# Output projection and Fourier feature products in scaled 16-bit halves, with the next layer's first weights made beside the projection

## The chip, the cores and the metric

The program runs on one core of a Trainium2 chip. The metric is the time of one execution on the device in microseconds (us); for a kernel it is the median of several runs. A profile is taken of one execution, and its span is the time from that execution's first instruction to its last. The engines are PE (TensorE: matmuls, with weight loads as PEld), DVE (VectorE), ACT (ScalarE), POOL (GpSimd) and SP (SyncE, which here issues every DMA).

## The reference

Two layers of a diffusion backbone run over 2048 latent tokens `x` and 256 context tokens `y`, with 1024 features. Each layer:

```
shift, scale, gate = split(silu(c) @ w_mod[l] + b_mod[l], 3)        # and the same from c_ctx for the context
h = rmsnorm(x, norm_g[l]) * (1 + scale) + shift
f_in, f_gate, g_u, g_v, g_gate, c_q, c_kv, k_rope, a_gate = split(h @ w_in[l])
f = (real(fft2(f_in by 4 groups of 64 features)) @ w_fmix[l]) * silu(f_gate)
g = spatial_gate(g_u, g_v) * silu(g_gate)                            # chunks of 128 tokens
o = attention(q(c_q), k, v(c_kv, k_rope)) * silu(a_gate)             # 8 heads, keys: context + latent
x = x + gate * (concat(f, g, o) @ w_out[l])                          # 256 + 256 + 512 features
```

The context takes the same step in the first layer only, with attention among itself. The output is `x` of the second layer, in 32-bit floats. `w_out` is 1024 x 1024 per layer, `w_fmix` 256 x 256, `w_mod` 1024 x 3072.

## The kernel before

The 2304 tokens are 18 tiles of 128 tokens (2 of the context, then 16 latent ones). Each operand of a matmul that must be exact is kept as a high and a low part, and a product is three matmuls: high x high, high x low, low x high (`mm3`, before line 682). For most of the kernel the parts are 16-bit floats: a matrix is first multiplied by a power of two that brings its largest entry near a fixed exponent (`power`, line 664, which needs a transpose, some tiny VectorE steps and a small matmul), then `halve` (line 866) makes the high part with two ScalarE passes and the low part with one POOL subtraction. The output projection and one step of the Fourier transform instead use pairs of 32-bit "f32r" tiles made by `split` (line 689): a ScalarE copy, and a subtraction on VectorE or POOL.

A layer has three stages:

1. Input projections, over blocks of two to six tiles. The columns of `w_in` are made into five weight groups (`group`, `resident`); group 0 holds keys and 416 columns, group 2 the gMLP's part. Each tile is normalised (`norm`) and transposed into 16-bit halves; the modulation is already multiplied into the small vectors `gs` and `sh`, made by `modulate_turned`, 64 VectorE operations for two of the three parts of `w_mod` (two conditions). Each takes 512 columns of a weight row and adds to an accumulator; `bounded` then fixes a power of two for the layer.
2. Attention over 8 heads, in steps of four query tiles. For each pair of key tiles a score matmul goes into PSUM, its maxima are scanned by VectorE, ScalarE takes two exponentials, POOL (three pieces of four) or VectorE (one of four) makes the low part, and PE multiplies by the values. Beside it a generator `background()` (line 1706) is advanced by fixed counts: first `fourier` (products by 64-point and 2048-point transforms, then by `w_fmix`), then the gate part (part 2) of `modulate_turned`, then `gates`, then `prepare` for the next layer.
3. The output stage. `weights()` (line 1005) loads `w_out` in two column halves of eight 128 x 512 pieces each through three buffers `wf`, and splits each to `wh` and `wl`. For each token tile, `mixed` (line 965) loads the concatenated mix from DRAM in three pieces into a buffer `k5`, transposes it (8 transposes in 2 groups, tiles `cb` and `cx`) and splits it. `outward` (line 1664) loads 512 columns of x, calls `project` (line 1027: 8 x 3 matmuls of 128 x 512 into a PSUM tile `pj`), multiplies by the gate, adds x and stores. Six tiles are made ahead (`XB`); between halves, two steps of the next layer's `modulate_turned` (parts 0 and 1) run, with 8 buffers `mw`.

The order of the instructions is not the order of the code. Every call is recorded and then a planner gives each engine a list in order of program priority, by an estimate of costs and by the number of free buffers in its pools; an instruction may be taken ahead of its place if its inputs and buffers are there. Each engine then runs its list strictly in that order, and all DMAs go through SyncE in 8 lanes. Every instruction is emitted by one line (448 before, 450 after), so the profile's rows are told apart by the names of tiles: `sc` scores, `pp` and `pw` exponentials, `pj` projections, `mw` weight rows of the modulation, `wf` raw pieces of `w_out`, `k` a general 32-bit buffer, `h` stacked halves (in the order also `h9`, `hp`).

Attention runs from 640 to 1427 us in layer 0 and from about 2180 to 2929 in layer 1; the output stages follow it, to 1686 and to the end.

Of the kernel before, what the change touches and what calls it, by code (L numbers as in the profile page):

```python
# [21 lines left out]
P = 128  # L22
D = 1024
# [38 lines left out]
XB = 6  # L62
# [4 lines left out]
PTOP, CTOP = 29, 14  # L67
# [482 lines left out]
def hybrid_kernel(ctx: ExitStack, tc: tile.TileContext, a: dict, out: bass.AP):  # L550
# [33 lines left out]
    def large():  # L584
        return mk(main, [P, T], F32R, "h9", 6)

# [3 lines left out]
    def k5():  # L590
        return mk(main, [P, NT * 65], F32, "k5")
# [96 lines left out]

    def split(hi, lo, x, leng=None):
        act.activation(out=hi, in_=x, func=AF.Copy)  # L690
        (leng or dve).tensor_tensor(out=lo, in0=x, in1=f(hi), op=ALU.subtract)
# [225 lines left out]
    def operand():  # L917
        h = large()
        parts = h[:, :2 * D].rearrange("p (s k n) -> p s k n", s=2, k=KC)
        return parts[:, 0], parts[:, 1]  # L920

# [42 lines left out]

    def mixed(t):
        xt = k5()[:, :D]
# [11 lines left out]
        return hh, hl  # L978
# [26 lines left out]
    def weights(parts, wp, scale=None, extra=None):  # L1005
        n = sum(c for _, c in parts)
        wt = []
        for k in range(KC):
            wf = mk(wp, [P, NB], F32, "wf", WF)[:, :n]
            c0 = 0  # L1010
            for get, c in parts:
                get(k, wf[:, c0:c0 + c])
                c0 += c
            if extra and k >= WB - KC:
                wh, wl = (mk(extra, [P, NB], F32R, s, 2 * KC - WB) for s in ("wh", "wl"))
            else:
                wh, wl = (mk(wp, [P, NB], F32R, s, WB)[:, :n] for s in ("wh", "wl"))
            if scale is not None and k >= 4:
                v = scale[:, k - 4:k - 3]
                act.activation(out=wh, in_=wf, func=AF.Copy, scale=v)  # L1020
                dve.scalar_tensor_tensor(out=wl, in0=wf, scalar=v, in1=f(wh), op0=ALU.mult, op1=ALU.subtract)
            else:
                split(wh, wl, wf, pool if k % 2 else dve)
            wt.append((wh, wl))
        return wt

    def project(ht, wt, n):
        o = bank(tag="pj")
        hh, hl = ht
# [242 lines left out]
    def fourier(l, y, pf):  # L1272
        back = mk(pf, [P, 1], F32, "back", 1)
        dve.tensor_scalar(out=back, in0=y["ic"][1], scalar1=2.0 ** (PTOP - CTOP), scalar2=None, op0=ALU.mult)
        fm = mk(pf, [P, 6, 256], F32R, "fm", 1)
        wfm = mk(pf, [P, 4, 256], F32, "wfm", 1)
        sp.dma_start(out=wfm, in_=a["w_fmix"][l].rearrange("k p n -> p k n"))
        first = wfm[:, 0]
        flip = column(C_FLIP)
        for s in range(3):  # L1280
# [4 lines left out]
            split(fm[:, 2 * s], fm[:, 2 * s + 1], first, pool)  # L1285
            yield

        def finish(re, im, cs, views):
# [22 lines left out]
            sh_ = [mk(pf, [P, 2, P], F32R, f"st{q}") for q in range(2)]  # L1311
            split(sh_[0], sh_[1], o)
            for gate_rows, out_rows, w in views:
                if w == 4:
                    sr_ = [mk(pf, [P, 2, P], F32R, f"sr{q}", 1) for q in range(2)]
                    for s, r in zip(sh_, sr_):
                        dve.tensor_copy(out=r, in_=f(s)[:, :, ::-1])
# [345 lines left out]
    def outward(l, y, t, n, ht, wt):  # L1663
# [6 lines left out]
        dve.tensor_tensor(out=o, in0=o, in1=y["gr"][1 if t < CT else 0][:, ns], op=ALU.mult)  # L1670
# [29 lines left out]
    for l in range(DEPTH):  # L1700
# [4 lines left out]
        def background():  # L1705
# [6 lines left out]
            load = lambda: mk(pools["W"], [P, NB], F32, "wh", WB)  # L1712
            for _ in modulate_turned(l, y, (2,), load):
                for _ in range(PACE):
                    yield
            gates(l, y, pools["C"])
# [162 lines left out]
```

## Time and profile before

| what | value |
|---|---|
| median of 3 runs | 3146.82 us (3145.03 to 3150.45) |
| profiled execution | 3142.39 us, span 3140.6 us |
| mean granted TensorE clock | 0.973 |
| DMA | 289.08 MB in 487,865 packets, 92 GB/s on average |
| HBM | 193.18 MB read, 91.66 MB written |

A row of a group gives the line, the engine, the operation, the output and inputs by name and shape, the count, then busy time in us and the mean ns of one, then the idle time of the engine just before them and what ended most of it. A row of the timeline gives the start, the duration and in square brackets the idle time before. A row of windows gives the length of a stretch, the busy time of each engine with its instruction count, the granted clock, the share of time in which a DMA engine was busy, and GB/s. "PEclk" is the TensorE clock that was granted, as a share of full speed.

### The profile page before, as it was taken

The numbers are of one execution on the slowest core, as the hardware profiler recorded it, in microseconds if no ns is written. First come the engines' busy times: TensorE is split into PE (matmuls) and PEld (weight loads), VectorE is DVE, ScalarE is ACT, GpSimd is POOL, SyncE is SP. The second block draws the span as 40 slices with busy tenths as digits, with TensorE's granted clock in tenths as the row PEclk, the third lists the DMA queues.
The fourth block names the chain that finished last, engine by engine and source line by source line (L and its number), as shares of the span: only waits on it lengthen the run. The fifth ranks groups of instructions, "written<-read, shape, count | busy, mean of one in ns | idle before, by whom it ended". The sixth has DMA issues, their size and how long they took to land.

```text
span 3140.6 us, 64404 instructions
## 1 busy us (share of the span) xinstructions
PE 2953.2 (94%) x23194; PEld 1724.2 (55%) x23194; DVE 2458.5 (78%) x6740; ACT 1826.3 (58%) x3904; POOL 1693.5 (54%) x1836
## 2 busy tenths in 40 slices
PE   6789999899999999998999999998999999999899
PEld 3445555445554555556785454553555555555687
DVE  7878788789999978765638888887899989887332
ACT  4553444167777788883006644531887887888400
POOL 3564444357667777772004744542876777777300
PEclk8899999999999999999999999998999999999999
DMA  7333344422324322205535343345023241230342
GB/s 271 69 73 58 84 94 87 102 88 67 86 61 131 81 72 61 57 23 177 175 118 192 62 86 86 87 96 142 24 64 79 71 125 49 61 75 20 111 134 81
DMA packets 487865, 289.08 MB, mean 92 GB/s; under 512 B 372316, under 2 KB 424180, under 8 KB 487544
## 3 DMA queue, kind: packets, MB, share of 16 engines
q1 hardware_dynamic: 487544, 284.96, 35.1%
q8 instruction: 182, 2.98, 0.4%
q14 instruction: 139, 1.14, 0.1%
HBM read 193.18 MB, written 91.66 MB: 91 GB/s over the span
## 4 chain that ended last, share of the span: by engine, by line
PE 59%; DVE 20%; DMA 8%; ACT 6%; POOL 3%; issue 2%; SPq 2%; DVEq 0%; ACTq 0%; POOLq 0%
PE pj L448 20%; PE sc L448 16%; PE pv L448 10%; PE mx L448 9%; DVE k L448 6%; DVE mx L448 4%; PE cb L448 3%; DMA k<-d 2%; ACT k L448 2%; SPq L448 2%; POOL k L448 2%; ACT pp L448 1%; DVE ns_t L448 1%; DMA mw<-in_w_modT_dram 1%; ACT pw L448 1%
## 5 line engine op out<-in xcount | busy, mean ns | idle before, releaser
L448 POOL TENSOR_TENSOR pp<-pw,pp 128x512 f16<-128x512 f32 (+1 forms) x876 | 1021.0, 1183 | 395.9 <-ACT pw L448 317.6
L448 PEld LDWEIGHTS <-h 128*128 128x128 f16 (+2 forms) x7008 | 581.8, 98 | 772.2 <-issue 410.2
L448 DVE TENSOR_REDUCE mx<-mx 128x1 f32<-128x512 f32 (+1 forms) x1296 | 770.9, 626 | 142.9 <-PE mx L448 136.9
L448 ACT ACTIVATE pp<-sc 128x512 f16<-128x512 f32 (+1 forms) x1168 | 717.5, 615 | 228.8 <-PE sc L448 215.5
L448 PE MATMUL sc<-h,h 128*128 128x512 f16 (+1 forms) x2336 | 602.8, 380 | 4.1 <-ACT pw L448 1.7
L448 ACT ACTIVATE pw<-sc 128x512 f32<-128x512 f32 (+1 forms) x876 | 543.7, 621 | 0.6 <-POOL pp L448 0.6
L448 PEld LDWEIGHTS <-pp 128*128 128x128 f16 x10432 | 467.3, 98 | 115.1 <-issue 32.5
L448 PE MATMUL pv<-k,pp 128*128 128x65 f16 (+2 forms) x10432 | 507.6, 203 | 7.6 <-DVE sm L448 7.0
L448 PE MATMUL mx<-h,h 96*128 96x512 f16 (+1 forms) x1296 | 410.4, 366 | 34.9 <-DVE mx L448 25.5
L448 PE MATMUL pj<-wh,h 128*128 128x512 f32 x1088 | 361.9, 405 | 7.3 <-DVE k L448 7.1
L448 PEld LDWEIGHTS <-hp 128*128 128x128 f16 x1920 | 187.8, 99 | 176.0 <-issue 14.3
L448 PE MATMUL pj<-w,h 128*128 128x512 f16 (+1 forms) x1296 | 272.2, 349 | 4.8 <-DVE tm L448 3.6
L448 PE MATMUL pj<-w,hp 128*128 128x512 f16 (+1 forms) x1152 | 241.4, 347 | 8.5 <-DVE tm L448 4.5
L448 POOL TENSOR_TENSOR h<-k,h 128x512 f16<-128x512 f32 (+1 forms) x72 | 80.8, 1138 | 299.6 <-ACT h L448 298.4
L448 PEld LDWEIGHTS pj<-wh,h 128*128 128x128 f32 x1088 | 208.6, 192 | 56.7 <-DVE k L448 11.1
L448 DVE TENSOR_TENSOR pp<-sc,pp 128x512 f16<-128x512 f32 (+1 forms) x292 | 197.8, 677 | 42.6 <-ACT sc L448 39.7
L448 PE MATMUL sc<-h 40*128 40x512 f16 (+1 forms) x1168 | 228.2, 387 | 0.0
L448 PE MATMUL pj<-wl,h 128*128 128x512 f32 x544 | 216.8, 399 | 0.0
L448 PE MATMUL pj<-h,h 128*128 128x416 f16 (+2 forms) x912 | 201.7, 363 | 6.5 <-ACT h L448 5.0
L448 DVE TENSOR_TENSOR pj<-pj,gr 128x512 f32<-128x512 f32 x68 | 47.3, 698 | 187.3 <-PE pj L448 187.3
L448 PE MATMUL pj<-h,hp 128*128 128x512 f16 (+1 forms) x768 | 174.4, 365 | 6.4 <-ACT hp L448 3.3
L448 ACT ACTIVATE sc<-sc 128x512 f32<-128x512 f32 (+1 forms) x292 | 178.8, 612 | 0.0
(270 smaller groups left out, 3936.7 us busy)
## 6 DMA issues: line engine op xcount, KB each, us to landing
d<-k SPq DMA_DIRECT2D x560, 48.0 KB
d<-k SPq DMA_DIRECT2D x166, 128.0 KB
d<-k SPq DMA_DIRECT2D x70, 256.0 KB
k<-d SPq DMA_DIRECT2D x132, 128.0 KB
k<-d SPq DMA_DIRECT2D x66, 256.0 KB
h<-d SPq DMA_DIRECT2D x24, 432.0 KB
d<-vt SPq DMA_DIRECT2D x144, 65.0 KB
k<-d SPq DMA_DIRECT2D x16, 585.0 KB
```

The lines of the kernel that those rows point to most:

```text
L448: r = getattr(getattr(self.nc, eng), method)(*args, **kw)
```

## The change

`weights()`, `operand()` and `split()` go. In their place:

- Weights of the output projection. `output_weights` runs at the end of `background()`, in attention: 16 loads of `w_out` pieces into one resident tile `wo` of 16-bit halves (each piece first sits there in full 32 bits), 16 VectorE maxima, `power`, then 16 `halve` calls. It is advanced once in three steps (`OPACE`).
- Tiles of the mix. `mixed` now scales each token tile by a power of two from its sum of squares: a ScalarE square with accumulation over 1024 columns, six VectorE steps on one column, a ScalarE scaling in place, then transposes as before and 16-bit halves, of two tiles in one `stacked` buffer. The inverse scale is applied in `outward`, in the operation that multiplies by the gate. The tiles made ahead fall from 6 to 4, the buffers `k5` rise from 2 to 3.
- The next layer. `onward` makes modulation parts 0 and 1 with 6 buffers `mw` in the pool W, `bounded`, and then the weight groups 0 and 2 in a new pool G, beside the output projection, in steps of 2 and 1 (`TICKS`) behind the two halves of a tile. All tiles do both halves in turn.
- Fourier. `w_fmix` is scaled and kept in 16-bit halves `fm`; the other operand `st` is 16-bit halves too, scaled by 2^-16. Its inverse scale is folded into `back`.

The core of the diff:

```diff
-TICKS = 2
+TICKS = 2, 1
+AHEAD_G = 2,
+OPACE = 3
-WB, WF = 11, 3
+WF = 3
-MW = 8
+MW = 6
-XB = 6
+XB = 4
...
     def k5():
-        return mk(main, [P, NT * 65], F32, "k5")
+        return mk(main, [P, NT * 65], F32, "k5", 3)
...
     def mixed(t):
         xt = k5()[:, :D]
...
-        hh, hl = operand()
+        ss = mk(small, [P, 1], F32, "ss")
+        act.activation(out=k2([P, D], BF16), in_=xt, func=AF.Square, accum_out=ss)
+        dve.tensor_scalar(out=ss, in0=ss, scalar1=2.0 ** -100, scalar2=2.0 ** 100, op0=ALU.max, op1=ALU.min)
+        pq = mk(small, [P, 2], F32, "mq", XB + 2)
...
+        dve.tensor_scalar(out=pq[:, 1:], in0=pq[:, 1:], scalar1=ow["pw"][:, 1:], scalar2=None, op0=ALU.mult)
+        act.activation(out=xt, in_=xt, func=AF.Copy, scale=pq[:, 0:1])
...
-            split(hh[:, 4 * half:4 * half + 4], hl[:, 4 * half:4 * half + 4], tp)
+            act.activation(out=hh[:, s], in_=tp, func=AF.Copy)
+            dve.tensor_tensor(out=hl[:, s], in0=tp, in1=hh[:, s], op=ALU.subtract)
...
-    def weights(parts, wp, scale=None, extra=None):
...
+    def output_weights(l, y, wp):
+        w = mk(wp, [P, KC, 2, 2, NB], F16, "wo", 1)
...
+                sp.dma_start(out=whole(w[:, k, n]), in_=a["w_out"][l, k * P:(k + 1) * P, n * NB:(n + 1) * NB])
+                dve.tensor_reduce(out=am[:, i:i + 1], in_=whole(w[:, k, n]), axis=AX.X, op=ALU.max, apply_absolute_value=True)
...
+                halve(w[:, k, n], r[:, max(0, k - 3):max(0, k - 3) + 1], mk(wp, [P, NB], F32, "wf", WF))
...
     def fourier(l, y, pf):
-        fm = mk(pf, [P, 6, 256], F32R, "fm", 1)
+        fm = mk(pf, [P, 6, 256], F16, "fm", 1)
+        power(am, fw, FTOP)
...
-            sh_ = [mk(pf, [P, 2, P], F32R, f"st{q}") for q in range(2)]
-            split(sh_[0], sh_[1], o)
+            sh_ = [mk(pf, [P, 2, P], F16, f"st{q}") for q in range(2)]
+            act.activation(out=sh_[0], in_=o, func=AF.Copy, scale=2.0 ** -STOP)
+            dve.scalar_tensor_tensor(out=sh_[1], in0=o, scalar=2.0 ** -STOP, in1=sh_[0], op0=ALU.mult, op1=ALU.subtract)
...
-        dve.tensor_tensor(out=o, in0=o, in1=y["gr"][1 if t < CT else 0][:, ns], op=ALU.mult)
+        dve.scalar_tensor_tensor(out=o, in0=o, scalar=ht[2], in1=y["gr"][1 if t < CT else 0][:, ns], op0=ALU.mult, op1=ALU.mult)
...
             gates(l, y, pools["C"])
+            for _ in output_weights(l, y, pools["W"]):
+                for _ in range(OPACE):
+                    yield
...
+        def onward():
+            for _ in modulate_turned(l + 1, nxt, (0, 1), lambda: mk(pools["W"], [P, NB], F32, "mw", MW)):
+                yield
+            bounded(nxt)
+            wt[0] = group(l + 1, nxt, 0, wp)
...
+            for g in AHEAD_G:
+                wt[g] = group(l + 1, nxt, g, wp)
...
-        for t in tiles[:-XB]:
+        if l < DEPTH - 1:
+            wp = opened("G", "left")
+            ahead = onward()
+        for t in tiles:
             for n in range(2):
-                outward(l, y, t, n, hts[t], wt[n])
-                for _ in range(TICKS):
+                outward(l, y, t, n, hts[t], ow["w"][n])
+                for _ in range(TICKS[n]):
                     next(ahead, None)
-            hts[t + XB] = mixed(t + XB)
+            if t + XB < NT:
+                hts[t + XB] = mixed(t + XB)
+            if l < DEPTH - 1 and t == NT - 3:
+                run(ahead)
```

The planner moves more than the diff shows. In the order of the changed program 50 of the 64 modulations of `onward`, with 25 of their 32 loads, stand inside the last two heads of layer 0's attention: about five in each step of four query tiles, then 7 and 12 in the last two steps; 14 are left for the output stage. Tiles 0 and 1 of the mix are loaded and partly transposed there as well, where before it was tile 0 alone. The modulation of part 2 and the maxima of `w_out` stand in the middle heads (steps 12 to 16 of layer 0's attention).

VectorE in the last head of layer 0's attention, before (`rc` and `sm` finish a step, `mx` are maxima of the scores, `pp` a low part):

```order
L448 RECIPROCAL rc_4406_21666<-pv_4334_21284 128x1
L448 RECIPROCAL rc_4406_21666<-pv_4334_21284 128x3
L448 TENSOR_TENSOR sm_4407_21669<-pv_4334_21284,sm_4407_21669 128x192
L448 TENSOR_REDUCE mx_4401_21632<-mx_4408_21672 128x1
L448 TENSOR_REDUCE mx_4401_21632<-mx_4410_21679 128x1
L448 TENSOR_TENSOR pp_4409_21676<-sc_4404_21657,pp_4409_21676 128x512
L448 TENSOR_REDUCE mx_4401_21632<-mx_4415_21697 128x1
L448 TENSOR_REDUCE mneg_4396_21621<-mx_4401_21632 128x1
L448 TENSOR_REDUCE mx_4421_21731<-mx_4419_21724 128x1
L448 TENSOR_REDUCE mx_4421_21731<-mx_4420_21729 128x1
```

And VectorE at the same place after; `mq` are the scales of the mix's tiles, `k2<-mw,mw` a piece of the next layer's modulation:

```order
L450 TENSOR_TENSOR pp_4443_21812<-sc_4436_21788,pp_4443_21812 128x512
L450 TENSOR_SCALAR mq_4421_21746<-mq_4421_21746,pwo_3323_16527 128x1
L450 TENSOR_SCALAR mq_4422_21748<-mq_4422_21748 128x1
L450 CAST mh_4451_21861<-mneg_4372_21481 128x4
L450 TENSOR_REDUCE mx_4438_21796<-mx_4450_21858 128x1
L450 CAST m8_4457_21897<-mh_4451_21861 128x4
L450 TENSOR_TENSOR m8_4457_21897<-mneg_4372_21481,mh_4451_21861 128x4
L450 TENSOR_REDUCE mx_4438_21796<-mx_4452_21863 128x1
L450 TENSOR_SCALAR mq_4422_21748<-mq_4422_21748,pwo_3323_16527 128x1
L450 SCALAR_TENSOR_TENSOR k2_4461_21910,acc_4000_19721<-mw_4383_21529,mw_3953_19527 128x512
L450 TENSOR_TENSOR h9_3913_19345<-cb_4460_21908,pick_6_165 8x512
L450 TENSOR_REDUCE mneg_4469_21951<-mx_4438_21796 128x1
```

The scales of two tiles and a modulation of 512 columns now stand between the maxima that the scores wait for.

PE at the boundary from layer 0 to layer 1, before (`cb<-ident,am` and `cb<-pe,ones` belong to `power`, `pj<-wh` and `pj<-wl` to the output projection, `pj<-h9,hp` to layer 1's first projection):

```order
L448 MATMUL cb_4867_24511<-ident_5_163,k5_4843_24319 128x128 x4
L448 MATMUL pj_4860_24435<-wh_4605_22830,h9_4810_23991 128x512
L448 MATMUL pj_4860_24435<-wl_4607_22837,h9_4810_23991 128x512
L448 MATMUL cx_4869_24523<-ident_5_163,k5_4843_24319 128x128 x4
L448 MATMUL cb_4877_24566<-ident_5_163,am_4844_24321 1x128
L448 MATMUL cb_4881_24594<-pe_4878_24569,ones_2_157 128x2
L448 MATMUL cb_4884_24605<-ident_5_163,am_4861_24459 1x128
L448 MATMUL cb_4892_24636<-pe_4887_24613,ones_2_157 128x2
L448 LDWEIGHTS hp_4873_24545
L448 MATMUL pj_4897_24651<-h9_4835_24272,hp_4873_24545 128x416
```

And after (`wo` is the resident weight, `h9` stacked halves):

```order
L450 MATMUL cb_4924_24857<-ident_5_163,k5_4881_24484 128x128 x4
L450 LDWEIGHTS h9_4862_24367
L450 MATMUL pj_4919_24793<-wo_2784_14020,h9_4862_24367 128x512
L450 MATMUL cx_4926_24869<-ident_5_163,k5_4881_24484 128x128 x4
L450 LDWEIGHTS h9_4902_24672
L450 MATMUL pj_4927_24875<-h9_4761_23626,h9_4902_24672 128x416
```

The two `power` steps that stood ahead of layer 1's first matmul are gone from this place; it follows a transpose of a normalised tile and the output projection's matmuls directly.

More of the change, by code (lines that the diff above doesn't have):

```diff
@@ L66 @@
 TOP = 14
-PTOP, CTOP = 29, 14
+PTOP, CTOP, STOP, FTOP = 29, 14, 16, 13
 KTOP = 11
@@ L963, in norm @@
         return hh, hl
+    mpair = [None]
     def mixed(t):
@@ L1003, in resident @@
         return [(v(k)[:, 0], v(k)[:, 1]) for k in range(KC)]
-    def weights(parts, wp, scale=None, extra=None):
-        n = sum(c for _, c in parts)
-        wt = []
+    ow = {}
+    def output_weights(l, y, wp):
+        w = mk(wp, [P, KC, 2, 2, NB], F16, "wo", 1)
+        am = mk(small, [P, 2 * KC + 1], F32, "wa", 1)
         for k in range(KC):
[L1009 to L1025, printed above, removed]
+            for n in range(2):
+                sp.dma_start(out=whole(w[:, k, n]), in_=a["w_out"][l, k * P:(k + 1) * P, n * NB:(n + 1) * NB])
+                i = 2 * k + n
+                dve.tensor_reduce(out=am[:, i:i + 1], in_=whole(w[:, k, n]), axis=AX.X, op=ALU.max, apply_absolute_value=True)
+                yield
+        late = am[:, KC:2 * KC].rearrange("p (k n) -> p k n", n=2)
+        dve.tensor_tensor(out=late, in0=late, in1=y["vinv"].unsqueeze(2).to_broadcast([P, 4, 2]), op=ALU.mult)
+        dve.tensor_reduce(out=am[:, 2 * KC:], in_=am[:, :2 * KC], axis=AX.X, op=ALU.max)
+        pw = mk(lay, [P, 2], F32, "pwo")
+        power(am[:, 2 * KC:], pw)
+        r = mk(small, [P, 5], F32, "wq", 1)
+        dve.tensor_copy(r[:, 0:1], pw[:, 0:1])
+        dve.tensor_scalar(out=r[:, 1:], in0=y["vinv"], scalar1=pw[:, 0:1], scalar2=None, op0=ALU.mult)
+        yield
+        for k in range(KC):
+            for n in range(2):
+                halve(w[:, k, n], r[:, max(0, k - 3):max(0, k - 3) + 1], mk(wp, [P, NB], F32, "wf", WF))
+                yield
+        ow["pw"] = pw
+        ow["w"] = [[(w[:, k, n, 0], w[:, k, n, 1]) for k in range(KC)] for n in range(2)]
@@ L1284, in fourier @@
             dve.tensor_tensor(out=first, in0=w, in1=z, op=ALU.subtract if s == 1 else ALU.add)
-            split(fm[:, 2 * s], fm[:, 2 * s + 1], first, pool)
+            act.activation(out=fm[:, 2 * s], in_=first, func=AF.Copy)
+            pool.tensor_tensor(out=fm[:, 2 * s + 1], in0=first, in1=fm[:, 2 * s], op=ALU.subtract)
             yield
@@ L1711, in background @@
             pools["C"] = opened("C", "right")
-            load = lambda: mk(pools["W"], [P, NB], F32, "wh", WB)
-            for _ in modulate_turned(l, y, (2,), load):
+            for _ in modulate_turned(l, y, (2,), lambda: mk(pools["W"], [P, NB], F32, "mw", MW)):
                 for _ in range(PACE):
@@ L1734, in hybrid_kernel @@
         plan.close(pa)
+        if l:
+            plan.close(wp)
         pools["B"] = opened("B", "left")
-        plan.close(wp)
+        if not l:
+            plan.close(wp)
         banks("scores")
```

63 lines of the change are left out of this document (31 added, 32 removed).

## The prediction

> **What bounds the kernel now.** I read the page first: the busy times, then the chain of work that ended last.
>
> ```profile
> span 3140.6 us, 64404 instructions
> PE 2953.2 (94%) x23194; PEld 1724.2 (55%) x23194; DVE 2458.5 (78%) x6740; ACT 1826.3 (58%) x3904; POOL 1693.5 (54%) x1836
> ...
> PE 59%; DVE 20%; DMA 8%; ACT 6%; POOL 3%; issue 2%; SPq 2%; DVEq 0%; ACTq 0%; POOLq 0%
> ```
>
> TensorE (PE) is busy for 94% of the span and carries 59% of the chain, so only two things pay: fewer PE microseconds, or less PE idle time. 187 us are idle in all, and where they lie decides the case. For that I went to the windows, PE alone (length, busy time with its matmuls, granted clock, DMA share, GB/s): the start of layer 0's output stage, the boundary to layer 1, the two places where `w_out` arrives during attention, and the start of layer 1's output stage.
>
> ```profile
> 1440.00:1560.00 120.00, 104.06 (x458) 0.93 0.64 199
> 1680.00:1700.00 20.00, 14.47 (x65) 0.74 0.96 337
> 1240.00:1280.00 40.00, 35.33 (x357) 0.91 0.59 159
> 2760.00:2800.00 40.00, 36.59 (x358) 0.96 0.36 88
> 2920.00:2960.00 40.00, 33.74 (x291) 0.91 0.39 118
> ```
>
> The idle time there is 15.9, 5.5, 4.7, 3.4 and 6.3 us. The third column adds to it: in each of these stretches the granted clock lies below 1.00, and a matmul is slower for it; (1 - clock) x length is my estimate of that loss, 8.4, 5.2, 3.6, 1.6 and 3.6 us. Next the timeline, for what ended the idle time (in square brackets).
>
> ```profile
> 1451.50 0.63 PE L448 MATMUL cx<-ident,k 128*128 128x128 f32 x4 [3.15 <-DMA k<-d]
> 1517.14 0.50 PE L448 MATMUL pj<-wh,h 128*128 128x512 f32 x1 [3.34 <-DVE k L448]
> 1683.04 0.58 PE L448 MATMUL cb<-pe,ones 1*128 1x2 f32 x2 [2.93 <-DVE pe L448]
> 1265.22 0.72 ACT L448 ACTIVATE wh<-wf,vinv 128x512 fp32r<-128x512 f32 x1 [5.07 <-DMA wf<-in_w_out_dram]
> 2770.26 0.63 ACT L448 ACTIVATE wh<-wf 128x512 fp32r<-128x512 f32 x1 [5.07 <-DMA wf<-in_w_out_dram]
> ...
>   DMA mw<-in_w_modT_dram: 14.4, 5
> ```
>
> Five reasons show: a tile of the mix that has not landed; VectorE's modulation of the next layer (its 14.4 us in 5 waits for rows of `w_modT` hold up everything queued behind it); the power of a weight group at the boundary; and ScalarE, in order, standing on a `w_out` load while softmax work is queued behind it. All five belong to work that the change moves. The rest of the kernel, the projections and the attention, is left as it is.
>
> **Part by part: what is gained.** First the rate of the output projection, 1088 + 544 = 1632 matmuls, now f32 and then f16. The chain has a long run of it that waits for nothing; the timeline has f16 matmuls of the same shape in the input projection, 18 of them from one start to the next row's.
>
> ```profile
> L448 PE MATMUL pj<-wh,h 128*128 128x512 f32 x1088 | 361.9, 405 | 7.3 <-DVE k L448 7.1
> L448 PE MATMUL pj<-wl,h 128*128 128x512 f32 x544 | 216.8, 399 | 0.0
> ...
> 3081.67 52.65 PE pj L448 x228
> ...
> 1756.14 4.05 PE L448 MATMUL pj<-w,hp 128*128 128x512 f16 x18
> 1760.02 0.81 PE L448 MATMUL pj<-w,h 128*128 128x512 f16 x3
> ...
> L448 PEld LDWEIGHTS pj<-wh,h 128*128 128x128 f32 x1088 | 208.6, 192 | 56.7 <-DVE k L448 11.1 <-ACT h L448 0.6 <-issue 0.5
> L448 PEld LDWEIGHTS <-h 128*128 128x128 f16 x4544 | 434.3, 99 | 393.2 <-issue 49.0 <-DVE tm L448 4.4 <-POOL h L448 1.5
> ```
>
> 52.65/228 is 0.2309 us a matmul before, 3.88/18 is 0.2156 after: 1632 x 0.0153 = **25 us** (20 if the f32 stream itself runs at 0.228 and the rest is transposes, 28 if some f16 streams do better). The mean ns of the group rows (405, 399) are modelled ends and overlap, so I don't use them. Weight loads halve, from 192 to 99 ns, but a 0.2309 us spacing already holds both a 0.192 load and a matmul, so they lie beside each other and the halving is worth nothing more.
>
> Layer 0's output stage: by the order of the changed program, 50 of the 64 modulations and 25 of their 32 loads go into attention and the weights are resident, so the DMA queue and VectorE are free for the mix's tiles. Of 15.9 + 8.4 = 24 us I take **18**. I leave 6 since a tile's way becomes longer: square, five to six tiny VectorE steps and a scaling now stand between its landing and its transposes, and only 3 tile buffers and 4 instead of 6 finished tiles run ahead. Ends 8 and 24.
>
> The boundary: group 0 and group 2 are made beside the projection, and the first `pj` of layer 1 stands right behind the last of layer 0. Of 5.5 + 5.2 = 10.7 us I take **8** (0 to 11), since the first norms still need the last stored rows of x. Layer 1's output stage: its weights are ready and two tiles transposed before attention ends; of 6.3 + 3.6 = 9.9 us I take **6** (0 to 10). What is late next in both is the first mix tile behind attention's last store, which the change does not touch.
>
> ScalarE's stalls on `w_out`: the first pass of the new weights is a VectorE maximum, and the halves come only once all 16 pieces are in SBUF, so ScalarE waits for no load. Of 4.7 + 3.6 + 3.4 + 1.6 = 13.3 us I take **10** (4 to 13), since VectorE, in order too, may now stand there for a piece.
>
> The Fourier products: a triple of 256 columns in f32r against the f16 of the same shape.
>
> ```profile
> 826.11 0.62 PE L448 MATMUL cb<-fm,st 128*128 128x256 f32 x3
> 826.57 0.39 PE L448 MATMUL mx<-h,h 96*128 96x512 f16 x1
> 826.61 0.71 PE L448 MATMUL cb<-fm,st 128*128 128x256 f32 x3
> 827.15 0.39 PE L448 MATMUL mx<-h,h 96*128 96x512 f16 x1
> ...
> 1746.83 2.97 PE L448 MATMUL pj<-w,h 128*128 128x256 f16 x24
> 1749.64 0.81 PE L448 MATMUL pj<-w,hp 128*128 128x512 f16 x3
> ...
> 840.00:880.00 40.00, 39.62 (x419) 21.86 (x418) 39.94 (x79) 34.05 (x75) 29.92 (x29) 1.00 0.48 114
> ```
>
> Two triples from start to next start take 0.46 and 0.54, mean 0.50; 24 f16 matmuls take 2.81, so a triple 0.35. 2 layers x 34 triples x 0.15 = 10 us. But they lie in the part of attention where VectorE is full (39.94 of 40, the third figure of the window) as well as PE, so I take half: **5** (0 to 12).
>
> **Part by part: what it costs.** The moved work goes into attention, where PE is full; it costs what it delays there.
>
> ```profile
> 960.00:1000.00 40.00, 19.86 (x90) 1.00 0.48 125
> 1320.00:1360.00 40.00, 22.56 (x104) 1.00 0.08 18
> 2600.00:2640.00 40.00, 22.14 (x100) 1.00 0.07 16
> ...
> 960.00:1000.00 40.00, 11.59 (x26) 1.00 0.48 125
> 2600.00:2640.00 40.00, 10.08 (x24) 1.00 0.07 16
> ...
> L448 DVE SCALAR_TENSOR_TENSOR k<-wh,wh 128x512 bf16<-128x512 f32 x64 | 58.6, 931 | 0.0
> L448 DVE SCALAR_TENSOR_TENSOR k<-mw,mw 128x512 bf16<-128x512 f32 x64 | 40.9, 686 | 17.3 <-DMA mw<-in_w_modT_dram 14.4 <-DMA d<-k 1.5 <-DMA wf<-in_w_out_dram 1.3
> L448 POOL TENSOR_TENSOR pp<-pw,pp 128x512 f16<-128x512 f32 x864 | 1012.8, 1189 | 364.6 <-ACT pw L448 286.3 <-PE pv L448 26.4 <-PE mx L448 13.7
> L448 DVE TENSOR_REDUCE am<-w 128x1 f32<-128x512 f32 x32 | 20.7, 671 | 0.4 <-DMA w<-in_w_g_dram 0.4
> L448 ACT ACTIVATE k<-k 128x1024 bf16<-128x1024 f32 x36 | 38.1, 1058 | 46.3 <-DMA k<-in_x_dram 17.2 <-DMA k<-d 15.8 <-DMA k<-in_ctx_dram 5.4
> ...
> 1320.00:1360.00 40.00, 40.00 (x422) 21.87 (x421) 31.61 (x71) 34.76 (x74) 30.46 (x32) 1.00 0.08 18
> 2880.00:2920.00 40.00, 39.82 (x454) 22.00 (x453) 17.03 (x36) 37.77 (x80) 33.06 (x32) 1.00 0.07 18
> ```
>
> The first three rows are the score matmuls (tile sc) in 40 us of attention: with nothing beside it 104, with modulation of the gate part beside it 90 and 100; the next two are that modulation on VectorE in the same stretches (half of the instructions read an accumulator), 13 and 12 pieces. So 14/104 x 40 = 5.4 us go with 13 pieces, 0.41 each, or 4/104 x 40 = 1.5 us with 12, 0.13 each. For the 50 moved modulations that is 6 to 21 us; **12** (outer ends 0, since VectorE has 8 us in 40 spare at 1320, and 50 x 1.0 = 50, if each costs its whole time).
>
> The 32 maxima of `w_out` (0.671 each, 21 us) and 64 small VectorE steps at the tiles take the place of 24 subtractions on VectorE; ScalarE makes two passes where it made one, and POOL the low half. At 0.13 for each maximum: **4** (0 to 15). And two more ScalarE passes of 1024 columns (1.058 us) for each of tiles 0 and 1 stand inside attention's end, where ScalarE is busy 37.77 of 40 us (last row): up to 2 x 4 x 1.06 = 8.5, **6**.
>
> Gains 25 + 18 + 8 + 6 + 10 + 5 = 72, costs 12 + 4 + 6 = 22, net 50. The profiled execution took 3142.39 us (1.8 more than its span), so 3092; the median of the runs stands 4.4 above it: **3097**.
>
> **Rivals.** *The waits come back.* With 3 tile buffers and a longer way for each tile, the output stages wait as before: 18 + 6 = 24 us are not won, 3121. For it speaks that tile landings ended some of the idle time at 1451; against it that the queue that delivered them carried the rows of `w_modT` and `w_out` beside them, most of which are gone from the stage.
>
> *Everything is covered.* The moved work fits into the spare 8 us of VectorE in each 40 and costs nothing: 22 us less, and half of the 13 us left in stages b, c and e goes too, 3068.
>
> *f16 is no faster here.* The 0.2309 is set by something else than the format (the read of the operands, the drain): terms of 25 and 5 vanish, 3127. The f16 rows speak against it.
>
> *Slower: VectorE stands on late rows in attention.* The moved modulations have 6 buffers, each conditioning row only 2 stream buffers, and all loads share SyncE's queue with attention's stores. In the output stage such a wait cost 14.4/5 = 2.9 us, and in attention the maxima that PE's scores need are queued behind it on VectorE. All 25 moved loads late: 72 us, 3169. It decides from 17 late loads on (17 x 2.9 eats the 50). Against it: the DMA share is 0.08 at 1320, so nothing should be late.
>
> *VectorE and POOL block each other.* The same operation takes 0.931 us on VectorE inside attention, with POOL at 1.189 us pieces beside it, and 0.686 outside it. If each moved modulation loses a whole POOL piece, 50 x 1.189 = 59 in place of 12: 3144, no change. [...]
>
> *Weight loads were never hidden.* If each matmul waits for its own load, f16 saves 1632 x (0.192 - 0.099) = 152 us in place of 25: 2970. [...]
>
> **How the numbers follow.** Forecast 0.55; everything covered 0.14; waits come back 0.13; late rows 0.08; blocking 0.05; f16 no faster 0.04; loads never hidden 0.01. The range takes in the first three, the f16 case and the better part of the unknown costs: **3058 to 3130**; left out are late rows, blocking and unhidden loads, 0.14. About 6 us (0.2%) is what a measurement of this kernel can tell from no change. Faster: 0.55 + 0.14 + 0.13 + 0.04 + 0.01 = 0.87; the same 0.05; slower 0.08.
>
> **What would show it.** The chain's long `pj` run near the end at 0.216 us a matmul shows the first term right, at 0.23 wrong. PE idle within 6 us in the first 120 us of layer 0's output stage and a granted clock of 1.00 there show the second. The boundary and layer 1's start each lose under 5 us. No ScalarE wait on `w_out`. Layer 0's attention should be longer by some 10 us in its last 200 us, and score matmuls should stay near 100 in 40 us there; under 90, or VectorE waits on `mw` in attention, would say that the moved modulation costs more than I allow. Attention's total longer by over 60 us would make the prediction wrong.

## The result: 3096.36 us, and the profile after

The changed kernel takes 3096.36 us (median of 4 runs, 3092.65 to 3099.93), the kernel before, beside it, 3145.93 (4 runs). The ratio is 0.9844, with a 95% interval of 0.9823 to 0.9865: 49.6 us less. The forecast was 3097. In the experiments below the kernel before, run again beside each, took 3148.20 or 3148.95 us, up to 3.0 more than here, so small differences of two totals are read from their ratios to it.

The page of the changed kernel, its first lines; the profiled execution took 3092.65 us:

```profile
span 3090.9 us, 64770 instructions
...
PE 2909.5 (94%) x23206; PEld 1564.8 (51%) x23206; DVE 2500.2 (81%) x6952; ACT 1921.5 (62%) x4040; POOL 1729.2 (56%) x1860
```

PE lost 43.7 us of busy time and its share stayed 94%; VectorE, ScalarE and POOL each do more. To see where the span became shorter I cut both executions at marks that the views of the tiles give: first and last start of a kind of matmul. The scores of the kernel before (tile sc; the two numbers after the durations are the first and the last start):

```profile
L448 PE MATMUL sc<-h,h x1184: 269/379/634, 639.0 to 1426.6; 128*128 128x512 f16 x192, 128*128 128x256 f16 x6
L448 PE MATMUL sc<-h,h x1152: 376/379/634, 2194.4 to 2928.4; 128*128 128x512 f16 x192
```

Its projections (tile pj; `wh` is the output projection, `h,hp` layer 1's first product):

```profile
L448 PE MATMUL pj<-wh,h x576: 387/393/796, 1430.6 to 1677.2; 128*128 128x512 f32 x192
L448 PE MATMUL pj<-h,hp x96: 339/379/551, 1686.8 to 1724.0; 128*128 128x416 f16 x48, 128*128 128x512 f16 x48
...
L448 PE MATMUL pj<-wh,h x512: 387/393/775, 2932.4 to 3135.3; 128*128 128x512 f32 x171
```

And the same after, scores first, then projections (`wo` is the output projection):

```profile
L450 PE MATMUL sc<-h,h x1184: 270/379/634, 626.3 to 1416.8; 128*128 128x512 f16 x192, 128*128 128x256 f16 x6
L450 PE MATMUL sc<-h,h x1152: 376/379/631, 2153.9 to 2893.1; 128*128 128x512 f16 x192
```

```profile
L450 PE MATMUL pj<-wo,h x864: 376/379/634, 1420.7 to 1640.5; 128*128 128x512 f16 x173
...
L450 PE MATMUL pj<-h,h x148: 339/339/379, 1641.2 to 1799.8; 128*128 128x416 f16 x96, 128*128 128x512 f16 x52
...
L450 PE MATMUL pj<-wo,h x768: 376/379/631, 2897.0 to 3085.8; 128*128 128x512 f16 x192
```

The differences of neighbouring marks are the stages. The same marks, read from the same two views of every kernel that ran, make this table (us, one profiled execution each):

| kernel | start to first score | attention 0 | output stage 0 | boundary | block 1 | attention 1 | output stage 1 to end |
|---|---|---|---|---|---|---|---|
| before | 639.0 | 791.6 | 246.6 | 9.6 | 507.6 | 738.0 | 208.2 |
| changed | 626.3 | 794.4 | 219.8 | 0.7 | 512.7 | 743.1 | 193.9 |
| k5_two | 639.4 | 793.0 | 226.0 | 0.8 | 496.7 | 741.5 | 200.9 |
| before_k5_three | 627.4 | 789.4 | 245.9 | 10.0 | 517.7 | 736.7 | 207.6 |
| mod_late | 624.3 | 781.3 | 236.0 | 0.6 | 512.5 | 744.8 | 196.0 |
| halves_slower | 628.8 | 782.1 | 226.2 | 0.6 | 514.7 | 737.7 | 195.8 |
| fourier_f32r | 624.4 | 797.3 | 220.0 | 0.7 | 513.0 | 746.1 | 192.7 |
| no_groups_ahead | 626.4 | 798.3 | 217.7 | 11.7 | 519.8 | 741.7 | 194.1 |
| only_halves_slower | 624.3 | 786.6 | 220.5 | 0.7 | 511.2 | 741.9 | 194.7 |
| norms_later | 626.3 | 784.2 | 223.8 | 0.6 | 573.5 | 736.3 | 195.5 |
| two_in_block | 628.3 | 783.0 | 224.2 | 0.8 | 497.6 | 743.1 | 195.0 |
| six_ahead | 626.0 | 781.4 | 224.0 | 0.2 | 507.6 | 737.6 | 199.3 |

The start is 624.3 to 628.8 in nine kernels that do not differ there, so this stage moves by some 4 us from one execution to another. I take that for the scatter of every stage, and do not read a difference of one stage below it.

From before to after: start -12.7, attention 0 +2.8, output stage 0 -26.8, boundary -8.9, block 1 +5.1, attention 1 +5.1, output stage 1 -14.3; the sum is the -49.7 of the spans. The first stage was not in the forecast at all.

The rate of the output projection, from the chain of waits after: a tile's 48 matmuls, and the long run at the end.

```profile
2965.06 10.45 PE pj L450 x48
...
3056.22 28.66 PE pj L450 x132
...
3056.22 29.95 PE L450 MATMUL pj<-wo,h 128*128 128x512 f16 x138 [0.15 <-DVE k L450]
```

That is 0.2177 and 0.2171 us a matmul, where before the long run had 0.2309. A row of the chain ends with the end of its last matmul and not with the start of the next, so such a mean is a little high. The last row, of the timeline, is the same run: without its last matmul's 0.38 us it takes 29.57 us for 137 steps from start to start, 0.2158 each. The same step taken on the run before gives (52.65 - 0.39)/227 = 0.2302. The windows of PE where the stages begin (length, busy, clock, DMA share, GB/s), and then output stage 0 as a whole, before and after:

```profile
1440.00:1560.00 120.00, 111.86 (x546) 0.99 0.54 166
1640.00:1660.00 20.00, 15.98 (x94) 1.00 0.30 95
2890.00:2930.00 40.00, 34.07 (x247) 0.96 0.43 129
...
1430.60:1677.20 246.60, 228.80 (x1052) 0.97 0.56 175
1420.70:1640.50 219.80, 208.89 (x1059) 0.99 0.58 185
```

From 1440 to 1560 us there are 8.1 us of idle time in place of 15.9, at a clock of 0.99 in place of 0.93; over the whole output stage 0, which begins 10 us earlier now, 10.9 in place of 17.8. At the boundary 4.0 us are idle (5.5 before), and at the start of output stage 1 5.9 (6.3 before): there almost no idle time went. What still ends idle time, from the timeline, with a row of ScalarE behind the first:

```profile
1445.31 0.65 PE L450 MATMUL cb<-ident,k 128*128 128x128 f32 x4 [3.27 <-ACT k L450]
1443.07 1.06 ACT L450 ACTIVATE k<-k 128x1024 bf16<-128x1024 f32 x1 [4.24 <-DMA k<-d]
...
1470.46 11.56 PE L450 MATMUL pj<-wo,h 128*128 128x512 f16 x45 [4.24 <-DVE k L450]
...
2907.74 0.81 PE L450 MATMUL cb<-ident,k 128*128 128x128 f32 x4 [2.94 <-ACT k L450]
```

Where PE waited for the landing of a tile before, it now waits for ScalarE's scaling of it (`ACT k`), one step later in the same tile's way. A landing is still behind the wait, but that of another tile. VectorE had made the scale by 1441.5 us; ScalarE, which works in order, stood until 1443.07 on the next tile's square, whose load had not landed, and did the scaling only after it, at 1444.12. At 2907.74 it is one tile's own way: its square had waited 4.16 us behind attention's last store. The wait at 1470.46 is for VectorE. Ahead of the two operations that free the projection's PSUM tile stand 1.34 us of waiting for such a square and 2.9 us of small steps, most of them of `bounded`.

In layer 0's attention the scores of two 40 us windows near its end (tile sc), first of the kernel before, then of the changed one, 680 to 760 us after the first score in each, and VectorE's waits in the last 200 us after:

```profile
1319.00:1359.00 40.00, 22.79 (x105) 1.00 0.08 18
1359.00:1399.00 40.00, 22.37 (x102) 1.00 0.09 23
...
1306.30:1346.30 40.00, 21.79 (x102) 1.00 0.19 54
1346.30:1386.30 40.00, 20.91 (x95) 1.00 0.15 46
```

```profile
DVE k L450 <- DMA mw<-in_w_modT_dram: 4.2, 1, 4.2
```

102 and 95 score matmuls in 40 us, where the kernel before had 105 and 102, and a single wait for a row of `w_modT` in the last 200 us of attention: the rows are not late.

### The profile page after: what moved, and what is told of

It is laid out like the page before. It is cut to its first block, busy times and chain, and to the rows that moved or that the text cites. A ratio compares the mean times of both kernels' runs of the same rounds, so it can differ in the third digit from the quotient of the medians.

```text
span 3090.9 us, 64770 instructions
## 1 busy us (share of the span) xinstructions
PE 2909.5 (94%) x23206; PEld 1564.8 (51%) x23206; DVE 2500.2 (81%) x6952; ACT 1921.5 (62%) x4040; POOL 1729.2 (56%) x1860
## 3 DMA queue, kind: packets, MB, share of 16 engines
q8 instruction: 182, 2.98, 0.4%
## 5 line engine op out<-in xcount | busy, mean ns | idle before, releaser
L450 PEld LDWEIGHTS <-h 128*128 128x128 f16 (+2 forms) x8640 | 742.2, 97 | 977.3 <-issue 435.8
L450 ACT ACTIVATE pp<-sc 128x512 f16<-128x512 f32 (+1 forms) x1168 | 748.2, 645 | 216.1 <-PE sc L450 201.9
L450 ACT ACTIVATE pw<-sc 128x512 f32<-128x512 f32 (+1 forms) x876 | 566.9, 651 | 0.1
L450 PE MATMUL pj<-wo,h 128*128 128x512 f16 x1632 | 365.6, 381 | 5.8 <-DVE k L450 5.8
L450 ACT ACTIVATE k<-k 128x768 f16<-128x768 f32 (+1 forms) x140 | 133.1, 951 | 239.8 <-DMA k<-d 120.3
L450 PEld LDWEIGHTS <-hp 128*128 128x128 f16 x1920 | 188.1, 99 | 166.8 <-issue 11.9
L450 ACT ACTIVATE sc<-sc 128x512 f32<-128x512 f32 (+1 forms) x292 | 187.9, 643 | 0.0
L450 PE MATMUL pj<-h,hp 128*128 128x416 f16 (+1 forms) x768 | 175.6, 363 | 6.8 <-ACT k L450 4.9
L450 ACT ACTIVATE k<-pj,pw 128x256 f32<-128x256 f32 (+4 forms) x208 | 93.1, 455 | 137.4 <-PE pj L450 124.8
L450 DVE STREAM_TRANSPOSE k<-k 128x384 f16<-128x384 f16 x280 | 144.5, 553 | 18.0 <-ACT k L450 12.7
```

The costliest lines, as they stand in the source:

```text
L450: r = getattr(getattr(self.nc, eng), method)(*args, **kw)
```

## The experiments

**The third tile buffer.** The start of layer 0 is 12.7 us shorter, and nothing in its code has changed. But the tiles of x that `norm` loads lie in the buffers `k5` too. Two kernels separate it.

```diff
 def k5():
-    return mk(main, [P, NT * 65], F32, "k5", 3)
+    return mk(main, [P, NT * 65], F32, "k5", 2)
```

> The changed kernel with two buffers k5 in place of three. The profile after has a gain that the prediction did not have: the first score matmul of layer 0 starts at 626.3 us, not 639.0, and the code of that stage was not changed, but the tiles of x that norm loads lie in k5. Theory (the third buffer made the start shorter): the first score matmul is back at 636 to 642, and layer 0's output stage (first to last projection matmul, 219.8 us) is 2 to 8 us longer, since a tile's load can run ahead less; in all 10 to 20 us slower than the changed kernel, 3106 to 3116. Rival (the start differs for another reason, the planner's order or the execution): first score matmul within 3 us of 626, total within 8 us of 3096.

Measured: 3105.67 us, ratio 0.9865 (0.9851 to 0.9879). Its scores, and its first product of layer 1:

```profile
L450 PE MATMUL sc<-h,h x1184: 269/379/634, 639.4 to 1429.0; 128*128 128x512 f16 x192, 128*128 128x256 f16 x6
L450 PE MATMUL sc<-h,h x1152: 376/379/634, 2155.9 to 2893.7; 128*128 128x512 f16 x192
```

```profile
L450 PE MATMUL pj<-h,h x48: 338/339/350, 1659.2 to 1679.5; 128*128 128x416 f16 x48
```

The theory holds: the start is back at 639.4, and the output stages are 6.2 and 7.0 us longer. But 13 + 6 + 7 = 26 us are lost and the total is only 9.3 longer, just under the forecast range (6.6 by the ratios). Block 1 gave 16.0 back (2155.9 - 1659.2 = 496.7).

The other way round, the kernel before with the third buffer:

```diff
 def k5():
-    return mk(main, [P, NT * 65], F32, "k5")
+    return mk(main, [P, NT * 65], F32, "k5", 3)
```

> The kernel before with three buffers k5 in place of two, and nothing else. Theory (the third buffer made the start shorter by itself): first score matmul at 624 to 630 in place of 639.0, the output stages 0 to 5 us shorter each, the rest as before: 3125 to 3135, ratio 0.993 to 0.997. Rival (the start differs for another reason): first score matmul within 3 us of 639, ratio within 0.002 of 1.

Measured: 3136.47 us, ratio 0.9965 (0.9951 to 0.9978).

```profile
L448 PE MATMUL sc<-h,h x1184: 270/379/634, 627.4 to 1413.3; 128*128 128x512 f16 x192, 128*128 128x256 f16 x6
```

The buffer alone makes the start 11.6 us shorter and block 1 10.1 us longer, and leaves the output stages where they were. The total is 1.5 us above the forecast range; the longer block was not in the forecast. That the output stages need the buffer only in the changed kernel fits the longer way of a tile there; no run tests this reason.

**The moved modulation.**

```diff
-for _ in modulate_turned(l + 1, nxt, (0, 1), lambda: mk(pools["W"], [P, NB], F32, "mw", MW)):
-    yield
+it = modulate_turned(l + 1, nxt, (0, 1), lambda: mk(pools["W"], [P, NB], F32, "mw", MW))
+while True:
+    plan.ahead = 40
+    more = next(it, 0)
+    plan.ahead = plan.AHEAD
+    if more == 0:
+        break
+    yield
```

> The changed kernel with the next layer's modulation held back in the planner, so that all 64 operations stand in the output stage and none in layer 0's attention. Theory (the prediction's: a moved modulation costs 0.13 to 0.41 us in attention, 12 us in all, and frees VectorE of the output stage): layer 0's attention (first score matmul to first projection matmul, 794.4) becomes 6 to 16 us shorter, the output stage of layer 0 (219.8) 12 to 30 longer, in all 3098 to 3115. Rival one (covered): attention within 3 us of 794, the output stage 15 to 30 longer, 3111 to 3126. Rival two (the moved work costs as much as it frees): total within 4 us of 3096.

Measured: 3099.31 us, ratio 0.9846 (0.9833 to 0.9859).

```profile
L450 PE MATMUL pj<-wo,h x864: 376/379/634, 1405.6 to 1641.6; 128*128 128x512 f16 x173
```

Attention 0 is 13.1 us shorter (781.3), 0.26 us for each of the 50 modulations, and output stage 0 16.2 longer (236.0). The price was 12 in the prediction. The move was a wash: by the two stages it frees 3 us more than it costs, and by the totals nothing (0.9846 against 0.9844). So the sizes of the theory held in the stages, and rival two in the total.

**The pace of the output weights.**

```diff
-OPACE = 3
+OPACE = 6
```

> The changed kernel with the output weights made at half the pace in attention (6 steps of the attention's loop for each piece in place of 3). In the profile after, layer 1's attention is 743.1 us, 5.1 longer than before, where the prediction had it 2.5 shorter, and ScalarE is busy 40.00 of 40 us from 2673.9, where the halves of the 16 pieces are made. Theory (two ScalarE passes for each piece in a burst fill ScalarE, and the exponentials are late): at half the pace layer 1's attention is 4 to 8 us shorter, layer 0's 2 to 8, in all 3082 to 3092. Rival (the passes cost their time at any pace, or something else makes attention longer): both attentions within 3 us, total within 5 us of 3096.

Measured: 3081.15 us, ratio 0.9785 (0.9772 to 0.9798), clearly faster than the changed kernel. Attention 1 is 5.4 us shorter, attention 0 12.3, of which a part is that only 44 modulations stand in it, not 50 (output stage 0 is 6.4 longer). All engines (PE, PEld, DVE, ACT, POOL, busy and count) where the 16 pieces are worked on in layer 1, in the changed kernel:

```profile
2593.90:2633.90 40.00, 36.41 (x339) 18.48 (x338) 37.43 (x78) 29.49 (x60) 25.46 (x23) 0.96 0.30 77
...
2673.90:2713.90 40.00, 37.38 (x378) 19.54 (x378) 31.11 (x65) 40.00 (x84) 37.56 (x37) 1.00 0.05 11
```

and at half the pace:

```profile
2592.40:2632.40 40.00, 38.55 (x415) 20.86 (x413) 38.40 (x94) 30.22 (x63) 26.36 (x24) 1.00 0.33 87
...
2752.40:2792.40 40.00, 39.82 (x425) 21.62 (x424) 32.30 (x67) 40.00 (x85) 37.37 (x35) 1.00 0.04 9
```

PE's idle time falls in both stretches, that of the maxima (36.41 to 38.55) and that of the halves (37.38 to 39.82). In the second ScalarE is still busy 40.00 of 40 us, and PE hardly waits: a full ScalarE alone was not the cost. To part the maxima from the halves, only the halves were slowed:

```diff
-for _ in output_weights(l, y, pools["W"]):
-    for _ in range(OPACE):
+for i, _ in enumerate(output_weights(l, y, pools["W"])):
+    for _ in range(OPACE if i < 16 else 6):
```

> The changed kernel with only the making of the halves of the output weights (two ScalarE passes and one POOL subtraction for each piece) at half the pace, the loads and maxima at the pace of the change. With both at half the pace layer 1's attention went from 743.1 to 737.7 us and the whole from 3096 to 3081. Theory one (ScalarE was too full): layer 1's attention 736 to 739, total 3079 to 3086. Theory two (the maxima crowd VectorE, in whose stretch from 2593.9 PE was busy only 36.41 of 40): layer 1's attention within 2 us of 743, total 3090 to 3098. Both in part: 739 to 741, 3086 to 3090.

Measured: 3085.00 us, ratio 0.9795 (0.9782 to 0.9808). The total falls into theory one, the 741.9 of attention 1 into theory two; the gain shows in attention 0 (786.6, 7.8 less). So the pace of the halves carries most of the gain of the total, but that it is ScalarE in layer 1 was not shown. What PE waits for says more. Its largest sum of waits in each attention is for VectorE to scan the maxima of the scores (`DVE mx`; us in total, times, longest), in attention 0 and 1 of the changed kernel, then with only the halves slower, then with all at half the pace:

```profile
PE mx L450 <- DVE mx L450: 18.5, 29, 4.1
PE mx L450 <- DVE mx L450: 8.9, 16, 2.3
...
PE mx L450 <- DVE mx L450: 13.1, 23, 3.9
PE mx L450 <- DVE mx L450: 8.4, 17, 2.3
...
PE mx L450 <- DVE mx L450: 10.9, 17, 4.6
PE mx L450 <- DVE mx L450: 5.3, 7, 2.8
```

In attention 0 these waits are 5.4 us less with slower halves and 7.6 less with both, where the stage is 7.8 and 12.3 shorter; in attention 1 0.5 and 3.6 less, where it is 1.2 and 5.4 shorter. This speaks for a hurry that reaches PE at least in part through VectorE's scans of the maxima; no run tests it alone. The gain in attention 1 does not come with half the pace alone: of the four kernels that have it three take 736.3 to 737.7 us there, and two_in_block takes 743.1.

**The Fourier products.** The change undone in `fourier`:

```diff
-fm = mk(pf, [P, 6, 256], F16, "fm", 1)
+fm = mk(pf, [P, 6, 256], F32R, "fm", 1)
...
-sh_ = [mk(pf, [P, 2, P], F16, f"st{q}") for q in range(2)]
+sh_ = [mk(pf, [P, 2, P], F32R, f"st{q}") for q in range(2)]
```

> The changed kernel with the Fourier feature products as before (f32r pairs, no scaling of w_fmix). Theory (the prediction's: 68 triples at 0.15 us less, half of it felt beside a full VectorE): the two attentions (794.4 and 743.1) are 5 us longer together, 0 to 12, so 3096 to 3108, taken 3101. Rival one (hidden): both attentions within 2 us. Rival two (the scaling's extra maximum, power and ScalarE pass cost more than the rate gains): attention shorter, 3088 to 3094.

Measured: 3099.37 us, ratio 0.9840 (0.9826 to 0.9853). The attentions are 2.9 and 3.0 us longer, 5.9 together where 5 was expected, but each alone lies within the scatter of a stage. The total is 3.0 us longer, and so was the kernel before beside it (3148.95 against 3145.93): the ratios, 0.9840 and 0.9844, do not differ. The products' gain is neither shown nor excluded.

**The weight groups made ahead.**

```diff
-AHEAD_G = 2,
+AHEAD_G = ()
...
-wt[0] = group(l + 1, nxt, 0, wp)
```

> The changed kernel without the weight groups 0 and 2 of the next layer beside the output projection: they are made in layer 1's block, as before; the modulation stays ahead. The prediction gave the boundary 8 us (0 to 11). But with two buffers k5 the boundary and layer 1's block together took 0.8 + 496.7 = 497.5 us, and 9.6 + 507.6 = 517.2 in the kernel before, 19.7 less; with three buffers 513.4. Theory (the groups are worth more than the boundary's idle time, 15 to 20): boundary and block together 528 to 534, layer 0's output stage 0 to 4 shorter, in all 3108 to 3116. The prediction's size: together 520 to 524, 3102 to 3106. Rival (nothing, the 19.7 come from elsewhere): within 4 us of 513.4 and of 3096.

Measured: 3113.80 us, ratio 0.9889 (0.9874 to 0.9904). Boundary and block take 11.7 + 519.8 = 531.5, 18.1 more. The timeline at the boundary shows the kernel before again, with two `power` steps on the path (`ident,am` and `pe,ones`):

```profile
1647.47 0.37 PE L450 MATMUL cb<-ident,am 128*1 128x128 f32 x1 [1.46 <-DVE k L450]
1650.83 0.58 PE L450 MATMUL cb<-pe,ones 1*128 1x2 f32 x2 [2.98 <-DVE pe L450]
```

By the stages the groups are worth 18 us, 11.0 at the boundary and 7.1 in the block; the total is 17.4 longer (14 by the ratios). A likely reason for the 7.1 is that the groups' maxima, passes and halves no longer stand among the first normalisations; no run tests it.

**Why the third buffer makes block 1 longer.** First try: hold back the loads of x in layer 1, with the output weights at half the pace.

```diff
 xt = k5()[:, :D]
+plan.ahead = 120 if l else plan.AHEAD
 sp.dma_start(out=xt, in_=src(l, t))
+plan.ahead = plan.AHEAD
```

> The changed kernel with the output weights at half the pace (3081.15 measured), and with the loads of x for layer 1's tiles held back in the planner (at most 120 operations ahead of the oldest that is open). Theory (the third k5 buffer makes layer 1's block 10 to 16 us longer, 512.7 against 496.7 and 517.7 against 507.6, because normalisations are taken early and crowd VectorE and ScalarE): the block 497 to 507, total 3066 to 3074. Rival (where the loads stand is not the cause): the block within 4 us of 514.7, or longer, total 3077 to 3090.

Measured: 3137.28 us, ratio 0.9964 (0.9951 to 0.9976); block 1 takes 573.5. The waits of PE in it, total, times and longest:

```profile
PE cb L450 <- DVE k L450: 28.8, 6, 9.5
PE pv L450 <- ACT vv L450: 18.8, 3, 9.1
```

`DVE k` before `cb` is the normalised tile that the transposes need: held back by this rule it comes too late, so my remedy was wrong. It does not test the theory, because it starves the block. The second try takes away the buffer itself, for the block alone:

```diff
+held[0] = k5()
+pool.memset(held[0][:, 0:1], 0.0)
 for u in BLOCKS[l + 1][0]:
...
 rs = rsqrt1(ss)
+if l and t == BLOCKS[l][-1][-1]:
+    dve.tensor_scalar(out=held[0][:, 0:1], in0=held[0][:, 0:1], scalar1=rs, scalar2=None, op0=ALU.mult)
```

> The changed kernel with the output weights at half the pace (3081.15 us measured, layer 1's block 514.7), and with one of the three buffers k5 held by a dummy tile (a memset of one column, one VectorE step on it at the last normalisation) while layer 1's block runs; elsewhere all three are free. The planned order of layer 1's normalisations is then that of two buffers. Holding back the loads instead made the block 573.5, so late loads are ruled out as a remedy. Theory (three buffers let normalisations be taken earlier in the block and that costs 10 to 16 us): block 496 to 504, start of layer 0 unchanged at 624 to 629, total 3064 to 3073. Rival (the block's length in the two-buffer kernel came from elsewhere, the output stage ahead of it or the attention behind): block 510 to 518, total 3077 to 3086.

Measured: 3070.12 us, ratio 0.9754 (0.9740 to 0.9768), the fastest kernel of this study, 26 us below the changed one. Its first product of layer 1, and its scores there:

```profile
L450 PE MATMUL pj<-h,h x64: 337/339/390, 1636.3 to 1680.0; 128*128 128x416 f16 x48, 128*128 128x512 f16 x16
```

```profile
L450 PE MATMUL sc<-h,h x1152: 376/379/634, 2133.9 to 2873.0; 128*128 128x512 f16 x192
```

2133.9 - 1636.3 = 497.6: without the third buffer the block is 17.1 us shorter, as the theory has it, and the start keeps its gain (628.3). Of the 17.1 the total shows 11.0, because attention 1 takes 743.1 us in place of 737.7; why is open. The buffer is the cause, but the theory's reason, normalisations that crowd VectorE, is not what the two traces show. The end of the block with three buffers (halves_slower), PE:

```profile
2136.51 0.81 PE L450 MATMUL pj<-w,h 128*128 128x512 f16 x3
...
2148.95 1.19 PE L450 MATMUL mx<-h,h 96*128 96x512 f16 x2 [0.36 <-DVE mx L450]
...
2152.21 0.37 PE L450 MATMUL cb<-ident,m 128*8 128x128 f32 x1 [1.52 <-DVE m L450]
```

and with two in the block:

```profile
2131.33 0.60 PE L450 MATMUL mx<-h,h 96*128 96x512 f16 x2
2133.78 0.27 PE L450 MATMUL cb<-ident,m 128*8 128x128 f32 x1 [1.85 <-DVE m L450]
```

The small matmuls `mx<-h,h` of 96 rows prepare the maxima of the first scores, and VectorE scans each. With three buffers 20 of them come after the last projection, one after another at VectorE's speed (in the changed kernel five of its scans take 2.98 us there, 0.60 each), and the first score starts 15.5 us behind the last projection (2136.9 to 2152.4). With two all but two of them stand among the projections or ahead of them, and the first score follows after 2.8 us (2131.1 to 2133.9). That is 12.7 of the 17.1. In the changed kernel and k5_two it is the same, 15.4 and 2.8. So the third buffer changes the order at the block's end; how it leads the planner to that order is open. In the kernel before, the gap is 15.8 us with two buffers and 15.4 with three, so the 10.1 us that its block loses lie elsewhere, and no run shows where.

**Six tiles ahead.**

```diff
-OPACE = 3
+OPACE = 6
...
-XB = 4
+XB = 6
```

> The changed kernel with the output weights at half the pace (3081.15 us), and six tiles of the mix made ahead in place of four. The prediction left 6 us in layer 0's output stage and 4 in layer 1's, since only 3 tile buffers and 4 instead of 6 finished tiles run ahead. Theory A (the finished tiles limit): the output stages (226.2 and 195.8) 3 to 8 us shorter each, total 3066 to 3075. Theory B (the way of a single tile from its load to its transposes limits, so tiles ahead change nothing): both within 3 us, total 3077 to 3085. Theory C (two more tiles' ScalarE passes move into attention's end): attentions longer by 2 to 6 each, total 3083 to 3093.

Measured: 3077.74 us, ratio 0.9777 (0.9764 to 0.9791). The output stages take 224.0 and 199.3, against 226.2 and 195.8: theory B holds, and the number of finished tiles is not what they wait for. What is left by the timeline is ScalarE's part of a tile's way, with the loads that it stands on; no run changed it. Block 1 is 7.1 us shorter here (507.6), although the three buffers stay: the gap ahead of the first score is 10.1 us in place of 15.5.

## Why the prediction was right, and where it was right by luck

The total was right to 1 us. By its own steps:

- *The rate, 25:* from 0.2309 to 0.2171 us in the long runs, 1632 x 0.0138 = 22.5 us; from start to start 0.2302 and 0.2158, 23.5 us. The mechanism held, at the rate of the input projection that the forecast took. The forecast's own 0.2309 carried the end of the run's last matmul, hence most of its 1.5 us too many.
- *Output stage 0, 18, and output stage 1, 6:* of -26.8 and -14.3 the rate takes 864 x 0.0138 = 11.9 and 768 x 0.0138 = 10.6, so 15 and 4 are left. I had left 6 and 4 us for the longer way of a tile; it is more. In stage 0 6.9 of the 15 are idle time, and some 5 are the higher clock, by the estimate (1 - clock) x length (7.4 us before, 2.2 after); in the kernel before a matmul of the projection took 0.43 us from start to start at a clock of 0.50 (1457.34 to 1459.47 us) and 0.23 at 1.00 (1442.56 to 1444.88). The sign that I named, under 6 us idle in the first 120 us and a clock of 1.00, was missed with 8.1 and 0.99. What I did not see is that the square makes ScalarE stand on the loads of the mix, with a finished tile's scaling behind it (1443.07), the kind of stall that I had named at `w_out`.
- *The boundary, 8, and nothing for block 1:* here the prediction failed. It priced the groups by the idle time at the boundary; no_groups_ahead shows 18. Against that stands the third buffer, which makes block 1 17 us longer (two_in_block). The two leave -3.8.
- *"The rest of the kernel, the projections and the attention, is left as it is":* this step was wrong. `k5` is one pool tag for the whole program; a third buffer moved the plan of both input stages. The start gained 12 us (k5_two, before_k5_three).
- *ScalarE's stalls, 10, the Fourier products, 5, the moved modulation, -12, maxima and halves, -4, the tiles' passes, -6:* together -7, and the two attentions are 7.9 us longer. Measured apart: modulation 13.1, and Fourier 5.9, which is not clear of the scatter; with both, the other three come to 13.1 - 5.9 - 7.9 = -0.7 gained together, where 10 - 4 - 6 = 0 was forecast. No run parts these three. And the pace test shows that this zero hides a cost: the weights made in a hurry cost some 15 us of the total, where the forecast had 4. It priced the maxima alone, and none of the small VectorE steps at the tiles; it counted 64 of these, the profile has five for each of 34 tiles, 170.

So the total came out by luck in part: what was missed on one side (12 us at the start) was nearly what was over-counted on the other (2.5 at the rate, 3 and 2 at the output stages, 4 at the boundary and block). Of the rivals, "f16 is no faster" is refuted by the rate (0.2302 to 0.2158 us a matmul), late rows by the 4.2 us of waits, and "everything is covered" by mod_late (its stages b, c and e are output stage 0, the boundary and output stage 1). "The waits come back" is refuted in output stage 0, where 6.9 us of idle time went; in output stage 1 it is nearly true, with 5.9 us idle at its start where there were 6.3. VectorE and POOL blocking each other is not excluded as a part of the 0.26 us of a moved modulation, but a whole POOL piece for each, 59 us, is. That weight loads were never hidden is refuted by the rate: in output stage 1 a load became 0.092 us shorter (190 to 98 ns), a matmul's step 0.0144.

## What to carry to other kernels

A change in the number of buffers of a shared tag is a change of every stage that uses the tag: list them all, and ask of each whether running ahead helps it (the start, a long single-tile way) or leads to a worse order of its work (block 1), because both signs were here, 12 us and 17. When work is moved into a full stage, the pace at which it is offered is a price of its own: the same work at half the pace was 15 us cheaper. And when a stage gets longer without more work, look at what stands just ahead of its last mark: here 12.7 of 17 us were small matmuls that had lost the projections that used to stand among them. And work made ahead of a boundary saves what it delays behind the boundary too, not only the idle time that the boundary shows.

## What the runs showed of the hardware

The same ScalarE pass over 512 columns, SBUF to SBUF, is slower inside attention. Groups of the changed kernel by form:

```profile
L450 ACT ACTIVATE wf<-wo,wq 128x512 f32<-128x512 f32 x32 | 30.9, 970 | 0.0
L450 ACT ACTIVATE wo<-wf 128x512 f16<-128x512 f32 x32 | 27.9, 875 | 0.0
...
L450 DVE SCALAR_TENSOR_TENSOR k<-mw,mw 128x512 bf16<-128x512 f32 x128 | 125.4, 993 | 17.6 <-DMA mw<-in_w_modT_dram 17.5
```

In the kernel before, the same two passes at the weight groups of the input projection, outside attention (the changed kernel has 712 and 621 there):

```profile
L448 ACT ACTIVATE k<-w,wr 128x512 f32<-128x512 f32 x32 | 21.4, 712 | 2.1 <-DVE wr L448 1.5 <-POOL w L448 0.5
...
L448 ACT ACTIVATE w<-k 128x512 f16<-128x512 f32 x32 | 18.5, 618 | 0.0
```

970 and 875 ns against 712 and 618: a quarter of a microsecond more for each pass. The modulation on VectorE goes the same way, 993 (a mean of which 16 of 128 lie in output stage 0) against 686 outside. But it does so unevenly: of the 80 that start in layer 0's attention of the changed kernel, the first 32 have a median of 689 ns and a longest of 1637, the other 48 a median of 1266 and a longest of 1653. What makes either engine slower there was not shown.
